# Eight modulation products at once: raising the adaLN units over a recurrence, and adding head sums low part first

## The chip, the cores and the metric

The kernel runs on one core of a Trainium2 chip. The metric is device time in microseconds (us), from the launch's start to its end on that core. A change of 0.3% is 4.9 us.

## The reference

One step of a diffusion backbone: 512 latent tokens and 128 context tokens of width 1024, one layer, all in float32. The layer is a mixer of three bidirectional recurrences (HGRN2, RWKV-7, mLSTM), each with a gated branch projection, and after it a SwiGLU; each half has an RMSNorm in front and behind. Cut to what the change touches:

```python
mod = (jax.nn.silu(cond) @ P['w_ada'][l] + P['b_ada'][l])[:, None, :]     # (2, 6 * 1024): c and c_ctx
sh1, sc1, g1, sh2, sc2, g2 = jnp.split(mod, 6, axis=-1)
h = _rms(x, nw[0]) * (1 + sc1) + sh1
y, st = _mixer(h, ...)                       # z = h @ W_in, 9616 columns, then the three recurrences
x = x + g1 * _rms(y, nw[1])
h = _rms(x, nw[2]) * (1 + sc2) + sh2
...                                          # SwiGLU, then x + g2 * _rms(y, nw[3])
# inside _rwkv7, sums over the 64 channels of each head:
kk = kk / jnp.maximum(jnp.sqrt(jnp.sum(kk * kk, axis=-1, keepdims=True)), 1e-12)
mean = jnp.mean(o, axis=-1, keepdims=True); var = jnp.mean(jnp.square(o - mean), axis=-1, keepdims=True)
bonus = jnp.sum(r_h * k_h * r_k, axis=-1, keepdims=True) * v_h
```

## The kernel before

**Layout and precision.** Channels lie on the 128 partitions, the 640 tokens on the free axis, in halves of 320. A projection of 128 output channels is a tile `pj` of one PSUM bank per token half; each of its 8 blocks of 128 input channels takes three single-pass matmuls (high by high, high by low, low by high parts, each rounded to `fp32r`), so a half has 24 of them.

**Modulation.** `sh1` and `sc1` are needed at once and are done before the mixer by `ada_first`. The other four vectors (32 of 48 blocks of 128 columns) are made by `ada_units`, 16 units of 256 columns, beside the recurrences. A unit loads two 512 KB pieces of `w_ada` (`raw`; the first holds input blocks 0 to 3, the second 4 to 7), and multiplies each of the eight blocks by a stationary of 32 columns (`sc32`, of which two count). Block k goes to quarter k % 4 of the PSUM tile `acc`, so that four products lie side by side in the array, in a shape of 128 x 32, and the second four add to the first. Each product is plain float32 and shows as two PE instructions in the profile: a unit has 16. ScalarE copies `acc` into `rows`, and `ada_columns` turns `rows` into columns and sums the quarters (`col_`, four PE instructions), one unit later.

**What shares a pool.** `acc`, `col_` and all projections take their banks from one pool, `pj`: two banks during the RWKV stage, four in the stage of the other two recurrences. `rows` shares two SBUF buffers (`gs`) with the gate projections, whose results go from `gs` to DRAM. The loads of the units share three `raw` buffers with all weights in the RWKV stage and have two of their own (`rawb`) in the next.

**Order.** Nothing here is queued by hand. A planner walks the program with its own model of times; on each engine it takes the ready instruction that stands earliest in the text. `tc.high_priority(n)` makes instructions count as n places earlier. The buffers and banks of one pool are handed out in the order of the text: in the compiled program all 408 tiles of `pj` are first written in that order. The RWKV chain (`rwkv`) runs 400 places up (`OFFD`), the projections ahead of it (`front_ahead`) and the filling work (`fill`) at their own places. `fill` follows `ORDER`: gate and output projections (h, o, g) with a unit (a) behind every two of them. `visit` keeps the many small matmuls of one chain step together on PE.

**Head sums.** `head_sum` sums over the 64 channels of a head by a matmul with a block matrix of ones, `bones`: ScalarE rounds the argument to `s_hi`, VectorE makes the rest, `s_lo`, and two matmuls add up in a tile `hs`. It is called eight times for each of the four head pairs, in `rwkv_front` and in `rwkv_post` (which runs raised), 32 times in all. Its bank is one of two that the chain's `lr`, `vtr` and `gg` tiles use too.

Of the kernel before, what the change touches and what calls it, by code (L numbers as in the profile page):

```python
# [49 lines left out]
SRATE = (0.3, 0.3, 0.3, 0.3)  # L50
OFFD = 400
OFFF = 0
HRATE = 2.0
KD = 8
C_DECAY = float(np.exp(-0.5))
# [200 lines left out]
def build(tc, **A):  # L256
# [19 lines left out]
    def mm(out, lhsT, rhs, start=True, stop=True, more=False):  # L276
        newest[0] = pe.matmul(out, lhsT=lhsT, rhs=rhs, start=start, stop=stop, skip_group_check=more).ins  # L277
# [12 lines left out]
    def f32(ap):  # L290
        return ap.bitcast(F32)

    with ExitStack() as top:
# [29 lines left out]
        def run(g):  # L323
            for _ in g:
                pass
# [4 lines left out]
        def wload(src, n=1024, pool_=None):  # L330
            raw = (raw_p if pool_ is None else pool_).tile([128, 1024], F32, name="raw")
            sp.dma_start(raw[:, :n], src)
            return raw
# [42 lines left out]
        def mixproj(name, x, evac):  # L376
            if name in loaded:
                wts, accs = loaded.pop(name)
                for n in range(2):
                    half_proj(wts, x, KD, n, evac, accs[n], range(4, KD))  # L380
                    yield
            else:
                yield from proj_steps(wsplit(A["wmix"][MIX_AT[name]]), x, KD, evac)

        def whole(g):

            n = sum(1 for _ in g)
            for _ in range(n):
                yield

        def half(t, n):
            return t[:, n * HN:(n + 1) * HN]
# [11 lines left out]
        sc32 = cp.tile([128, KD, 32], F32, name="sc32")  # L404
        pool.memset(sc32, 0.0)
        pool.tensor_copy(sc32[:, :, 0:2], sc)

        def ada_part(acc, raw, k0, w):


            for a in range(1024 // w):
                k = k0 + a
                q = slice(32 * (k % 4), 32 * (k % 4) + 32)
                mm(acc[q], sc32[:, k], raw[:, a * w:a * w + w], k < 4, k >= 4)

        def ada_columns(o, rows, n):

            col_ = pj_p[0].tile([128, 4, 2], F32, name="col_", tag="pj")
            for m in range(n):
                mm(col_[:, m], rows[:, m * 128:m * 128 + 128], cols[:, COL_SEL:COL_SEL + 2])  # L420
            tt(mod[:, o:o + n], col_[:, :n], P("b_ada", o, n).unsqueeze(2).to_broadcast([128, n, 2]), ALU.add)
# [81 lines left out]
        bones = mc_p.tile([128, 128], F32R, name="bones")  # L503
# [36 lines left out]
        def weave(*streams):  # L540

            live = [[g, r, 0.0] for g, r in streams]
            while live:
                x = min(live, key=lambda a: a[2])
                try:
                    next(x[0])
                    x[2] += 1.0 / x[1]
                    yield
                except StopIteration:
                    live.remove(x)  # L550
# [13 lines left out]
        def fill():  # L564

            def to_dram(i, name, raw=False):
                def ev(acc, n):
                    gs = gt_p.tile([128, HN], F32, name="gs")
                    if raw:
                        act.copy(gs, acc)  # L570
                    else:
                        act.activation(gs, acc, AF.Tanh, scale=0.5)
                    sp.dma_start(half(gates[i], n), gs)
                yield from whole(mixproj(name, h, ev))
                filled.add(i)

            def ada_units():

                last = None
                for u in range(16):  # L580
                    acc = pj_p[0].tile([128, 256], F32, name="acc", tag="pj")
                    for b in range(2):
                        ada_part(acc, wload(A["wada"][16 + 2 * u + b], pool_=ada_raw[0]), 4 * b, 256)
                    if last:
                        ada_columns(*last)
                    rows = gt_p.tile([128, HN], F32, name="rows", tag="gs")
                    act.copy(rows[:, :256], acc)
                    last = (16 + 2 * u, rows, 2)
                    yield
                ada_columns(*last)  # L590
                yield

            au = ada_units()
            todo = {"g": [(b * 8 + m, f"g{b}_{m}") for b in range(3) for m in range(8)],
                    "h": [(28 + i, f"hg{i}", True) for i in range(4)],
                    "o": [(24 + i, f"mo{i}") for i in range(4)], }
            for x in ORDER:
                if x == "a":
                    yield next(au)
                else:  # L600
                    yield from to_dram(*todo[x].pop(0))
            assert not any(todo.values())
            yield from au

        ada_raw = [raw_p]
# [3 lines left out]
        def first(g, offset):  # L609

            while True:
                try:
                    if offset:
                        with tc.high_priority(offset):
                            next(g)
                    else:
                        next(g)
                except StopIteration:
                    return
                yield  # L620

        def run_over(main, under, rate):

            a = 0.0
            for _ in main:
                a += rate[at[0]]
                while a >= 1.0:
                    a -= 1.0
                    next(under, None)
# [5 lines left out]
        with ExitStack() as rs:  # L635
# [296 lines left out]
            def head_sum(b, eng):  # L932

                hi = tp.tile([128, HN], F32R, name="s_hi", bufs=1)
                lo = tp.tile([128, HN], F32R, name="s_lo", bufs=1)
                act.copy(hi, b)
                eng.tensor_tensor(lo, b, f32(hi), ALU.subtract)
                acc = ps.tile([128, HN], F32, name="hs", tag="A")
                mm(acc, bones, hi, True, False)
                mm(acc, bones, lo, False, True)  # L940
                return acc

            def rwkv_front(p, R):
# [16 lines left out]
                for n in range(2):  # L960
                    ts(half(nkk, n), head_sum(half(t1, n), HE), 1e-24, op0=ALU.max)
# [21 lines left out]
                for n in range(2):  # L983
                    mul(half(yb, n), head_sum(half(t2, n), HE), half(v, n))
# [30 lines left out]
            def front_ahead():  # L1015

                for x in fr:
                    yield
                    while at[0] < 3 and Rs[at[0] + 1].get("ready"):
                        yield  # L1020
# [9 lines left out]
            def rwkv():  # L1030
                last = None
                for p in range(4):
                    while not Rs[p].get("ready"):
                        yield next(fr)
                    at[0] = p
                    elem, prepare, scan = rwkv_pair(p, Rs[p])
                    for gi in range(3):
                        g = chain(elem(), prepare(0)) if gi == 0 else prepare(gi)
                        yield from weave((last, SRATE[p]), (g, 1.0)) if last else g
                        last = scan(gi)  # L1040
                        if gi == 2:
                            last = chain(last, finish(p))
                yield from last

            run_over(weave((first(rwkv(), OFFD), 1.0), (first(front_ahead(), OFFF), FRONT)), fl, FILL)

        with ExitStack() as ms, ExitStack() as mr:
# [288 lines left out]
            def mlstm():  # L1336
                yield from mlstm_gates()
                mr.close()
                mt = ms.enter_context(tc.tile_pool(name="mt", bufs=2, reuse_waits="tile"))
                for hd in range(4):  # L1340
                    at[0] = hd
                    yield from mlstm_head(hd, mt)
# [89 lines left out]
            def hgrn():  # L1432
                for hd in range(4):
                    yield from hgrn_head(hd)

            at[0] = 0
            run_over(weave((mlstm(), 1.0), (hgrn(), HRATE)), fl, FILL2)
            run(fl)
# [106 lines left out]
        def ff1_tiles():  # L1545
            return ft.tile([128, T], F32, name="u"), ft.tile([128, T], F32, name="sg")
# [240 lines left out]
        for c, js in enumerate(CHUNKS):  # L1787
# [3 lines left out]
            if c == 0:  # L1791
# [3 lines left out]
                u, sg = ff1_tiles()  # L1795
# [38 lines left out]
```

## Time and profile before

| | us |
|---|---|
| median of the runs shown (1621.6 to 1626.25, three runs) | 1624.72 |
| the profiled execution's own time | 1626.68 |
| its span, from the first to the last instruction | 1624.9 |
| PE busy in the span | 1550.9 (95%) |
| VectorE, ScalarE, GpSimd busy | 1104.1, 802.4, 276.3 |

The span is 1.8 us short of the execution's own time, and that execution lies 2.0 us above the median. PE means matmuls, PEld weight loads, which can run beside them. A matmul's record covers its way through the array, so records overlap; what one instruction costs is read better from the start of one to the start of the next. SP issues the loads; its rows say when, not for how long a transfer ran.

### The profile page before, as it was taken

To read this page: it belongs to the slowest core of one execution; us is meant where nothing else is said; L and a number is where in the kernel's file an instruction comes from. 1 tells how busy PE (TensorE), PEld (TensorE's weight loads), DVE (VectorE), ACT (ScalarE), POOL (GpSimd) and SP (SyncE) were. 2 spreads that over 40 slices of the span, in tenths; PEclk is the share of its full clock that TensorE was granted. 3 is DMA by queue.
4 is the path that set the end of the run, shared out by engine and by line. 5 is a ranking of instruction groups with operands and counts; after the bars stand their busy time and mean duration, and the time that the engine had idled before them with its cause. 6 is when DMAs were issued, how large, how long until landed. Compare 5 with 4: busy or idle time off the path is not lost. (4 is left out here: it accounts for less than half of the span.)

```text
span 1624.9 us, 36010 instructions
## 1 busy us (share of the span) xinstructions
PE 1550.9 (95%) x14834; PEld 1424.6 (88%) x14834; DVE 1104.1 (68%) x2307; ACT 802.4 (49%) x1594; POOL 276.3 (17%) x347
## 2 busy tenths in 40 slices
PE   5999999999999998899999999999999999999996
PEld 2988878878877888889798988999999999999996
DVE  5787767676677544686858678772887386586576
ACT  5354555364455354756476666223553443343244
POOL 1110111110110110221303021000123241341211
PEclk9999999999999999999999999999989999999998
DMA  9221212222223232232332333643512222222322
GB/s 351 81 71 62 83 58 76 68 82 74 67 72 100 88 132 87 61 105 80 90 101 85 99 103 97 200 143 110 156 37 85 95 79 75 82 89 69 102 96 88
DMA packets 63796, 157.43 MB, mean 97 GB/s; under 512 B 7432, under 2 KB 27912, under 8 KB 63504
## 3 DMA queue, kind: packets, MB, share of 16 engines
q1 hardware_dynamic: 63488, 155.13, 29.7%
q8 instruction: 116, 1.90, 0.5%
q14 instruction: 48, 0.39, 0.1%
q10 hardware_dynamic: 144, 0.00, 0.0%
HBM read 136.73 MB, written 18.37 MB: 95 GB/s over the span
## 5 line engine op out<-in xcount | busy, mean ns | idle before, releaser
L277 PE MATMUL pj<-h_hi,whi 128*128 128x320 f32 x1560 | 494.9, 320 | 5.9 <-ACT t L396 2.9
L277 PE MATMUL pj<-h_hi,wlo 128*128 128x320 f32 x1560 | 493.8, 317 | 0.0
L277 PE MATMUL pj<-h_lo,whi 128*128 128x320 f32 x1560 | 493.5, 317 | 0.0
L262 DVE TENSOR_TENSOR wlo<-raw,whi 128x512 fp32r<-128x512 f32 (+1 forms) x318 | 228.4, 726 | 129.8 <-ACT whi L344 104.5
L277 PEld LDWEIGHTS pj<-h_hi,whi 128*128 128x128 f32 x1560 | 295.1, 190 | 13.0 <-ACT t L396 4.2
L277 PEld LDWEIGHTS pj<-h_hi,wlo 128*128 128x128 f32 x1560 | 295.7, 190 | 3.6
L277 PEld LDWEIGHTS pj<-h_lo,whi 128*128 128x128 f32 x1560 | 295.8, 190 | 3.2
L344 ACT CAST whi<-raw 128x512 fp32r<-128x512 f32 (+1 forms) x264 | 156.9, 600 | 215.4 <-PE pj L277 200.8
L277 PE MATMUL pj<-a,whi 128*128 128x320 f32 x704 | 155.3, 309 | 0.0
L277 PEld LDWEIGHTS pj<-a,whi 128*128 128x128 f32 x704 | 117.7, 188 | 0.2
L277 PE MATMUL pj<-a,wlo 128*128 128x320 f32 x352 | 108.8, 309 | 0.0
L277 PE MATMUL pj<-t_hi,whi 128*128 128x320 f32 x288 | 89.1, 309 | 1.1 <-DVE u L262 1.1
L277 PE MATMUL pj<-t_hi,wlo 128*128 128x320 f32 x288 | 89.1, 309 | 0.4 <-DVE wlo L262 0.4
L277 PE MATMUL pj<-t_lo,whi 128*128 128x320 f32 x288 | 89.0, 309 | 0.0
L1686 ACT CAST whi<-sm 128x512 fp32r<-128x512 f32 x72 | 44.4, 621 | 64.5 <-PE pj L277 50.2
L262 DVE TENSOR_TENSOR wlo<-sm,whi 128x512 fp32r<-128x512 f32 x72 | 68.0, 946 | 11.6 <-ACT whi L1686 8.6
L1680 POOL TENSOR_TENSOR sm<-raw 128x512 f32<-128x512 f32 x36 | 48.4, 1346 | 110.7 <-DMA raw<-wff 72.9
L277 PEld LDWEIGHTS pj<-a,wlo 128*128 128x128 f32 x352 | 66.1, 188 | 0.0
L277 PE MATMUL pj<-hl,whi 128*128 128x320 f32 x256 | 56.5, 310 | 0.6 <-ACT hl L1464 0.6
L807 DVE CAST_PREDICATED E<-msk,q 128x512 f16<-128x512 uint8 (+1 forms) x60 | 35.9, 598 | 30.3 <-PE q L277 30.2
L277 PE MATMUL acc<-raw,sc 128*32 128x256 f32 (+1 forms) x320 | 42.1, 454 | 15.0 <-DMA raw<-wada 15.0
L1686 ACT CAST whi<-raw 128x512 fp32r<-128x512 f32 x54 | 33.5, 621 | 45.6 <-PE pj L277 37.7
(661 smaller groups left out, 3029.2 us busy)
## 6 DMA issues: line engine op xcount, KB each, us to landing
raw<-wmix SPq DMA_DIRECT2D x76, 512.0 KB, 3.8
raw<-wada SPq DMA_DIRECT2D x48, 512.0 KB, 4.6
raw<-wff SPq DMA_DIRECT2D x44, 512.0 KB, 3.8
gates<-gs SPq DMA_DIRECT2D x64, 160.0 KB, 1.7
raw<-wff SPq DMA_DIRECT2D x24, 384.0 KB, 3.2
gs<-gates SPq DMA_DIRECT2D x24, 320.0 KB, 3.0
raw<-wbr SPq DMA_DIRECT2D x12, 512.0 KB, 4.0
raw<-wout SPq DMA_DIRECT2D x8, 512.0 KB, 5.0
```

The costliest lines, as they stand in the source:

```text
L262: dve.tensor_tensor(out, a, b, op)
L277: newest[0] = pe.matmul(out, lhsT=lhsT, rhs=rhs, start=start, stop=stop, skip_group_check=more).ins
L344: act.copy(hi[:, :w], raw[:, o:o + w])
L807: dve.copy_predicated(E[l][:, :, :n], mki(l), q[:, :, :n])
L1680: pool.tensor_tensor(o, x, y, op)
L1686: act.copy(hi, x)
```

## The change

The two loads of a unit are both issued ahead of its products. The products then run in one block that counts as 1000 places earlier (the chain has 400): first the four of the second load, which now start the sums, then the four of the first. The copy to `rows` and `ada_columns` keep their places. In `head_sum` the two matmuls change places: the low part starts the sum, the high part ends it. The amount of work is the same. `ada_first` calls `ada_part` as before.

```diff
+OFFA = 1000
@@
-        def ada_part(acc, raw, k0, w):
+        def ada_part(acc, raw, k0, w, first=None):
             for a in range(1024 // w):
                 k = k0 + a
                 q = slice(32 * (k % 4), 32 * (k % 4) + 32)
-                mm(acc[q], sc32[:, k], raw[:, a * w:a * w + w], k < 4, k >= 4)
+                start = k < 4 if first is None else first
+                mm(acc[q], sc32[:, k], raw[:, a * w:a * w + w], start, not start)
@@ ada_units
                     acc = pj_p[0].tile([128, 256], F32, name="acc", tag="pj")
-                    for b in range(2):
-                        ada_part(acc, wload(A["wada"][16 + 2 * u + b], pool_=ada_raw[0]), 4 * b, 256)
+                    parts = [wload(A["wada"][16 + 2 * u + b], pool_=ada_raw[0]) for b in range(2)]
+
+                    with tc.high_priority(OFFA):
+                        for b in (1, 0):
+                            ada_part(acc, parts[b], 4 * b, 256, b == 1)
                     if last:
                         ada_columns(*last)
                     rows = gt_p.tile([128, HN], F32, name="rows", tag="gs")
@@ head_sum
                 acc = ps.tile([128, HN], F32, name="hs", tag="A")
-                mm(acc, bones, hi, True, False)
-                mm(acc, bones, lo, False, True)
+                mm(acc, bones, lo, True, False)
+                mm(acc, bones, hi, False, True)
```

## Rows read from the trace of the kernel before

**Rows 1.** The page: busy time of each engine, and one group of PE instructions (count, then busy us and mean ns of one, then idle time before them).

```profile
PE 1550.9 (95%) x14834; PEld 1424.6 (88%) x14834; DVE 1104.1 (68%) x2307; ACT 802.4 (49%) x1594; POOL 276.3 (17%) x347
...
L277 PE MATMUL acc<-raw,sc 128*32 128x256 f32 (+1 forms) x320 | 42.1, 454 | 15.0 <-DMA raw<-wada 15.0
```

**Rows 2.** Busy time by stage: about the RWKV stage, the HGRN and mLSTM stage, and the rest. Columns: the stretch, its length, busy us (and instructions) of PE, PEld, DVE, ACT and POOL, granted clock, share and GB/s of the DMA engines.

```profile
100.00:600.00 500.00, 490.71 (x6594) 404.29 (x6593) 340.56 (x838) 251.20 (x512) 65.87 (x144) 1.00 0.24 78
600.00:1010.00 410.00, 385.26 (x3742) 363.79 (x3741) 289.70 (x629) 256.45 (x508) 71.86 (x80) 0.99 0.30 92
1010.00:1624.90 614.90, 594.85 (x4025) 591.24 (x4024) 406.39 (x707) 248.82 (x492) 124.28 (x96) 0.97 0.32 101
```

**Rows 3.** The same view, of the instructions that write or read `acc` alone, one stretch for each of the 16 units. Columns: the stretch, its length, busy us of PE (16 instructions each), PEld and ACT, clock, DMA. The last row sums all 16.

```profile
135.00:138.00 3.00, 1.68 (x16) 0.54 (x16) 0.37 (x1) 1.00 0.09 15
...
390.00:392.00 2.00, 1.07 (x16) 0.42 (x16) 0.05 (x1) 1.00 0.14 18
451.00:454.20 3.20, 1.89 (x16) 0.44 (x16) 0.37 (x1) 1.00 0.26 27
483.00:490.50 7.50, 2.29 (x16) 0.67 (x16) 0.30 (x1) 1.00 0.06 22
...
1001.00:1003.00 2.00, 1.07 (x16) 0.42 (x16) 0.00 (x0) 1.00 0.00 0
sum 80.10, PE 27.29 PEld 8.06 ACT 2.19; mean PE 1.71 PEld 0.50 ACT 0.14
```

**Rows 4.** The timeline of PE in the RWKV stage around a unit. Columns: start, us, engine, line, operation, tiles, shape, count, and in brackets the idle time before.

```profile
450.91 0.30 PE L277 MATMUL pj<-h_hi,wlo 128*128 128x320 f32 x1
451.14 0.62 PE L277 MATMUL acc<-raw,sc 128*32 128x256 f32 x2
451.69 0.31 PE L277 MATMUL xp<-c,Y 64*64 64x64 f16 x8
451.93 0.64 PE L277 MATMUL acc<-raw,sc 128*32 128x256 f32 x8
452.50 0.68 PE L277 MATMUL rr<-Xf,NA 64*64 64x64 f32 x16
453.12 0.63 PE L277 MATMUL acc<-raw,sc 128*32 128x256 f32 x6
453.68 0.61 PE L277 MATMUL col__6030<-cols,rows 128*128 128x2 f32 x4
```

**Rows 5.** The timeline of PE around the last unit, in the same columns.

```profile
1001.09 0.31 PE L277 MATMUL pj<-h_lo,whi 128*128 128x320 f32 x1
1001.24 0.31 PE L277 MATMUL pj<-h_hi,wlo 128*128 128x320 f32 x1
1001.48 1.07 PE L277 MATMUL acc<-raw,sc 128*32 128x256 f32 x16
1002.48 0.61 PE L277 MATMUL col__13893<-cols,rows 128*128 128x2 f32 x4
```

**Rows 6.** The timeline of SP: when the loads of the unit of rows 7 were issued; and how long the 48 loads of `w_ada` took to land.

```profile
522.88 0.33 SPq L332 DMA_DIRECT2D raw<-wada  x1
...
524.88 0.33 SPq L332 DMA_DIRECT2D raw<-wada  x1
```
```profile
DMA to landing us min/median/max: 3.5/4.6/10.2
```

**Rows 7.** The timelines of PE, of ScalarE and of VectorE around one unit of the RWKV stage that stands behind a gate projection.

```profile
557.29 0.39 PE L277 MATMUL pj<-h_hi,wlo 128*128 128x320 f32 x1
557.61 0.62 PE L277 MATMUL acc<-raw,sc 128*32 128x256 f32 x2
558.16 0.45 PE L277 MATMUL z<-zs,Yf 64*64 64x64 f32 x8
558.54 1.06 PE L277 MATMUL acc<-raw,sc 128*32 128x256 f32 x14
559.53 0.61 PE L277 MATMUL col__8195<-cols,rows 128*128 128x2 f32 x4
560.60 0.41 PE L277 MATMUL pj<-h_hi,whi 128*128 128x320 f32 x1 [0.46 <-ACT rows L587]
```
```profile
557.84 0.44 ACT L572 ACTIVATE gs<-pj 128x320 f32<-128x320 f32 x1
560.18 0.37 ACT L587 COPY rows<-acc 128x256 f32<-128x256 f32 x1 [1.90 <-PE col__8195 L277]
```
```profile
560.18 0.16 DVE L262 TENSOR_TENSOR mod<-col__8195,pcol 128x4 f32<-128x4 f32 x1 [0.92 <-PE col__8195 L277]
```

**Rows 8.** The timeline of PE around a head sum; one group of VectorE instructions (ns: least, median, most); and one row of the waits of PE (us in total, times, longest).

```profile
401.27 0.41 PE L277 MATMUL hs<-s_hi,bones 128*128 128x320 f32 x1 [0.25 <-ACT s_hi L936]
401.61 0.37 PE L277 MATMUL y<-Y,E 64*64 64x64 f16 x11
401.92 0.41 PE L277 MATMUL hs<-s_lo,bones 128*128 128x320 f32 x1
402.26 0.24 PE L277 MATMUL y<-Y,E 64*64 64x64 f16 x3
```
```profile
L937 DVE TENSOR_TENSOR s_lo<-t,s_hi x24: 450/491/561, 85.5 to 596.6; 128x320 fp32r<-128x320 f32 x24
```
```profile
PE hs L277 <- ACT s_hi L936: 0.4, 2, 0.3
```

## The prediction

> **What bounds the kernel now.** First the busy times of the page [rows 1]: PE is busy 1550.9 of 1624.9 us, the next engine, VectorE, 1104.1. Then the same by stage [rows 2]. The changed instructions lie in the first two stretches: the RWKV stage, where PE lacks 500 - 490.7 = 9.3 us of being always busy, and the next stage, where it lacks 24.7. So there is little waiting to remove, and a change gains only if PE gets the same products done in less time. That this is possible shows in two columns: in the RWKV stage matmuls are busy 490.7 us but weight loads only 404.3, while after 1010 us both are near 594. In the RWKV stage something stands between the matmuls that counts as busy.
>
> What it is shows when the starts of neighbours are compared. Inside a half projection the next matmul starts 0.15 us later ([rows 5], 1001.09 to 1001.24). From the last `pj` matmul to the first of `acc` it is 0.24 (1001.24 to 1001.48). A whole unit in one piece takes 1.00 until the next instruction starts (1001.48 to 1002.48). In [rows 4] a unit is cut into three: 0.55, 0.57 and 0.56 from each piece's start to the start of the foreign work behind it, 1.68 in all. Two instructions cost over half of what sixteen cost together, so most of a piece is the price of getting out of the array's 128 x 32 shape.
>
> **The change, part by part.**
>
> *The loads.* Both are already issued well before they are needed: the pair of [rows 6] at 522.88 and 524.88, with a landing time of 4.6 us in the median and 10.2 at most, for products that start at 557.61 [rows 7]. Starting from the later load and issuing both first therefore costs and gains 0. The cover is some 20 us of lead; without it PE would stand up to 10.2 us at a unit, and nothing in the change removes it, since loads keep their place in the text.
>
> *The products in one piece.* [Rows 3] has the PE time of each unit: 1.07 where it ran whole (two units, at 390 and 1001), 1.68 in two pieces, 1.89 in three, 2.29 in the worst, together 27.29. Sixteen whole units would take 16 x 1.07 = 17.12, which leaves 10.17. A piece's record overlaps the next instruction by 0.07 (451.14 + 0.62 against 451.69), and by their busy times the units have some 36 pieces, 20 more than 16: 20 x 0.07 = 1.4 is no gain. So joining them is worth 10.2 - 1.4 = 8.8 us if no unit is cut any more. It should not be: once the first product can go, the other seven are ready and stand 1000 places up, ahead of the chain's 400. Bounds: 0 if other work still gets between, 8.8.
>
> The Trainium skill ("TensorEngine Tiling (Array Packing)", Key Properties) has a reason for the 0.5 us: a change of tiling mode drains the engine. It gives no price; by it a piece between two kinds of work whose modes differ anyway would save one drain of two, and the sum would be half, 4.4 (a time of 1622.4, a rival below). The rows speak against half: in [rows 4] two `acc` instructions take 0.55 and eight take 0.57, so the price hangs on the exit from `acc`, not on the products, and it goes with the piece.
>
> *Where the products go.* Today all products stand behind the last matmul of the half projection before them, because its matmuls are earlier in the text. At 1000 places up they go as soon as a bank of `pj` is free. In the RWKV stage there are two banks: the one of the first half comes free when that half is evicted, early in the second half. So the products move into the middle of the second half. That takes away a cover. Today they fill the time in which ScalarE evicts the second half: in [rows 7] the eviction ends at 557.84 + 0.44 = 558.28, and PE could go on at 557.61, so 0.67 us is covered. After the change that time belongs to `col_`, which is next in the text for a bank, and it must wait; then the next projection waits for a bank from `col_` (VectorE ends at 560.34, 0.81 after the start of `col_`, of which PE works 0.61) or from `rows`. New uncovered time: 0.67 + 0.20 = 0.87 a unit. The chain's small matmuls fill part of it: `z` holds 0.38 (558.16 to 558.54) of the 0.93 from 557.61 to 558.54, and `xp` and `rr` in [rows 4] are more, so I take half. Eleven units lie in the RWKV stage; six of them stand behind a gate projection, whose `gs` buffer also holds up `rows`, and five behind a projection of the chain, where `rows` can be copied early and the bank is back in time. I take 6 x 0.87 x 0.5 = 2.6, with 0.4 for the five others: 3. Bounds: 0, since today's wait for `rows` (0.46 in [rows 7]) may go with it, and 11 x 0.87 = 9.6 if nothing fills it. The five units of the second stage have four banks and lose nothing.
>
> *Head sums.* The low part is ready one VectorE instruction (0.49 us, [rows 8]) after the high part. Today PE takes the high part as soon as it is there, turns to other work and comes back: in [rows 8] each of the two visits inside the group `y` takes 0.34 until `y` goes on, against 0.15 for a matmul among its like. With the low part first, both are ready when the first goes, so one visit serves both. A visit saved is worth 0.34 - 0.15 = 0.19 or a little more (its way in), and about nothing where the neighbours are `pj`. Read in the same way, 20 of the 32 pairs stand apart in the timeline; at some 0.12 each that is 2.5 us. Bounds: 0, and 20 x 0.19 = 3.8. The bank is taken later and for a shorter time, and `s_hi` is held about 0.5 us longer; the next head sum waits for that, but its 0.5 us lies under PE's other work.
>
> *Sum.* -8.8 + 3 - 2.5 = -8.3 us of PE time, in stages where PE is 94 to 98% busy. The whole order behind the first moved instruction is planned anew, so the 34 us of idle time in these stages may shift by a few us either way; some products that now fall into waits will do so no more. I take -7: the profiled execution's 1626.7 would become 1619.7. It lies 2.0 above the median of the runs, so the median goes from 1624.7 to about 1618.
>
> **The rivals.**
>
> *The full gain, 1612:* no uncovered time and all visits gone, 1624.7 - 8.8 - 3.8. For it: PE shows hardly any wait for banks today. Against: the bank of `acc` is held longer than now.
>
> *No change, 1624:* the products go together, but what they saved is lost again where PE has no bank to write to (bubble of 0.87 little filled, 8 to 9 us) or the new order leaves other pieces cut. For it: two banks, and the wait of 0.46 that is already there. The change not doing what it says, with units still cut, ends here too, and so does the skill's half gain (1622.4, 0.04 of the chance).
>
> *Slower, 1633:* the two banks block each other. `acc` sits in one from the middle of the second half until `rows` is copied, and `rows` needs a `gs` buffer, of which the unit before holds one; the other bank waits for its eviction. If PE stood 1.8 us (0.99 from 557.29 until the eviction's end, and the 0.81 of `col_`) at each of eleven units, that is 19.8 against gains of 11.3, so 1624.7 + 8.5. It decides from 11.3 / 11 = 1.03 us a unit on. Against it: the chain always had matmuls to give around a unit (`xp`, `rr` and `z` in [rows 4, 7]). The Trainium skill ("TensorEngine Tiling (Array Packing)", PSUM Bottleneck) warns of this kind of thing: packing speeds up the products, not the eviction.
>
> *PE stands at the low part, 1632:* the queue of PE holds at a matmul whose operand is late, and the low part is 0.49 later than the high one: 32 x 0.49 = 15.7, less the 8.8 of the products: 1624.7 + 6.9. Against it: PE waited 0.4 us in all at head sums for `s_hi` [rows 8], and the planner places them by when both parts are ready. The Trainium skill ("TensorE: Matmul & The Clock Gate", Part 3, The mechanism) says that matmuls stay in order.
>
> **How the numbers follow.** Forecast (1613 to 1622, most likely 1618) 0.52, full gain 0.06, no change 0.24, banks blocked 0.13, low part late 0.05. What a measurement can tell from no change is 0.3%, 4.9 us: faster is below 1619.8. Of the forecast some four fifths lie there, with the full gain 0.48 and a little of "no change": 0.5. Same: a fifth of the forecast and most of "no change", 0.31. Slower: 0.19, the last two and a rest. The range, 1611 to 1630, leaves out the lower end of the full gain and the worse half of the slower cases.
>
> **What the profile after would show.** Right: `acc` in 16 rows of x16, each about 1.07, sum near 17.1 in the view of [rows 3]; `pj` matmuls of one half on both sides of them in the RWKV stage; `s_lo` directly followed by `s_hi`; PE busy down by some 10 us, its idle time between 100 and 1010 us up by 2 to 4. Wrong: `acc` still in pieces; `pj` or `col_` in the RWKV stage with idle time behind ScalarE's `gs` or `rows` of over 0.5 us at most units; waits of `hs` on `s_lo`; a longer gap between the stages near 650 us.

## The result, and the profile after

The change made the kernel slower: 1636.43 us in the median (8 runs) against 1624.38 for the kernel before, beside it, a ratio of 1.0076 with an interval of 1.0057 to 1.0096. That is 12 us in place of the 7 us of gain forecast, and above the range. The profiled execution after took 1636.35 us, with a span of 1634.5.

The first view is of the products alone, one stretch for each unit, as in [rows 3] (a unit in the middle, and the sum):

```profile
452.00:455.00 3.00, 1.07 (x16) 0.42 (x16) 0.37 (x1) 1.00 0.23 45
...
sum 141.00, PE 17.13 PEld 6.68 ACT 5.59; mean PE 1.07 PEld 0.42 ACT 0.35
```

All sixteen units run whole, in 1.07 us, together 17.13 where [rows 3] has 27.29. The head sums do what was forecast, too: PE's timeline around one (against [rows 8]), and what PE waits for at them in the whole run.

```profile
342.01 0.31 PE L278 MATMUL hs<-s_lo,bones 128*128 128x320 f32 x1
342.16 0.31 PE L278 MATMUL hs<-s_hi,bones 128*128 128x320 f32 x1
```
```profile
PE hs L278 <- DVE s_lo L942: 0.9, 3, 0.4
```

25 of the 32 pairs now stand next to each other (11 before), and waiting for the low part costs 0.9 us in all. So the work has become less, as it should. The page's line for PE and the busy time by stage (as [rows 1] and [rows 2], the same stretches up to 1010 us) show what else happened:

```profile
PE 1545.6 (95%) x14834; PEld 1430.2 (87%) x14834; DVE 1106.9 (68%) x2307; ACT 801.4 (49%) x1594; POOL 278.4 (17%) x347
```
```profile
100.00:600.00 500.00, 483.11 (x6567) 405.21 (x6566) 339.99 (x836) 246.82 (x506) 67.73 (x144) 0.99 0.24 75
600.00:1010.00 410.00, 381.06 (x3722) 361.99 (x3721) 282.70 (x603) 249.82 (x489) 72.43 (x80) 0.98 0.29 91
```

PE's idle time grew from 9.3 to 16.9 us in the RWKV stage and from 24.7 to 28.9 in the next, and the granted clock fell by 0.01 in both. The trace records the clock as stretches at full or at half speed; up to the start of the last stage (the first write of `x1d`, at 1138.9 us before and at 1149.1 after) half-speed stretches last 20.5 us before and 41.0 after. At half speed half the time is lost, which gives an account of the 10.2 us:

| up to the first `x1d` | before | after | difference |
|---|---|---|---|
| time | 1138.9 | 1149.1 | +10.2 |
| PE idle, 100 to 1010 us | 34.0 | 45.8 | +11.8 |
| half of the time at half clock | 10.2 | 20.5 | +10.3 |
| the rest: PE's work at full clock, and its idle time outside 100 to 1010 us | 1094.7 | 1082.8 | -11.9 |

(Each column is one execution, and idle time at half clock counts twice, so each row is good to some 2 us. With all idle time up to the first `x1d`, 54.6 and 68.8, and only busy time at half clock, the differences are +14.1 idle, +10.4 clock and -14.3 work.) The work saved is at least what the prediction said, 8.8 + 2.5 = 11.3. It was paid back by idle time, for which the prediction had 3, and then lost once more to the clock, for which it had nothing. The runs bear the clock out: over 29 runs of the kernel before, the time falls by 1.03 us for each 0.001 of mean granted clock. Its mean was 0.986 in those runs, and 0.979 in the eight of the changed kernel: about 7 of the 12 us.

Where does it happen? First in the RWKV stage, at the unit that starts at 332 us (unit 4). The timeline of PE, that of ScalarE, and the stretches before and after the pause (columns as in [rows 4], [rows 7] and [rows 2]):

```profile
332.41 1.07 PE L278 MATMUL acc<-raw,sc 128*32 128x256 f32 x16
...
343.33 0.31 PE L278 MATMUL pj<-h_hi,wlo 128*128 128x320 f32 x1
344.96 1.16 PE L278 MATMUL p<-AX,BK 64*128 64x128 f32 x8 [1.32 <-DVE BK L263]
346.05 0.80 PE L278 MATMUL col__4607<-cols,rows 128*128 128x2 f32 x4
346.77 2.08 PE L278 MATMUL p<-AX,BK 64*128 64x128 f32 x8
```
```profile
344.81 0.42 ACT L574 ACTIVATE gs<-pj 128x320 f32<-128x320 f32 x1
...
346.88 0.37 ACT L592 COPY rows<-acc 128x256 f32<-128x256 f32 x1 [1.03 <-PE col__4607 L278]
```
```profile
332.00:346.30 14.30, 12.97 (x97) 8.78 (x95) 10.84 (x25) 9.43 (x19) 3.11 (x6) 1.00 0.36 118
346.30:360.00 13.70, 13.70 (x79) 12.12 (x79) 9.04 (x24) 3.96 (x8) 1.65 (x5) 0.50 0.02 7
```

Three things are to be seen. The products ran at 332.41, in the middle of the second half; their result left the bank at 346.88, 14.5 us later, because `rows` got no `gs` buffer: the copy waits for `col__4607`, which reads the `rows` of the unit before. Behind the second half (its last `pj` is at 343.33) the chain is not ready, since VectorE is late with `BK`, and PE has nothing to put in: 1.32 us idle. And from 346.3 the clock is granted at 0.50, 1.2 of 2.4 GHz, for 13.7 us: eight matmuls `p` take 2.08 in place of 1.16.

Second, in the HGRN and mLSTM stage, at units 12 and 14. Unit 12, ScalarE, PE, and the stretch behind it:

```profile
784.42 0.44 ACT L574 ACTIVATE gs<-pj 128x320 f32<-128x320 f32 x1 [3.38 <-DMA gates<-gs]
784.75 0.58 ACT L1145 COPY hkt<-htr 128x512 f32<-128x512 f32 x1
```
```profile
781.90 0.31 PE L278 MATMUL pj<-h_lo,whi 128*128 128x320 f32 x1
785.39 1.16 PE L278 MATMUL hpr<-hv,hkt 128*128 128x128 f32 x8 [3.18 <-ACT hkt L1145]
```
```profile
786.70:790.00 3.30, 3.30 (x18) 3.30 (x17) 2.83 (x7) 1.66 (x4) 1.65 (x2) 0.50 0.38 144
```

The second half's `gs` stands in ScalarE's queue in front of the chain's `hkt`, and waits 3.38 us until the DMA of the `gs` before it has left the buffer. PE waits 3.18 for `hkt`, and the clock is at half behind that. At unit 14 it is the same (3.21, 3.02, half clock from 974.4). In the kernel before, `hkt` stands in front of that `gs` (ScalarE at the same unit):

```profile
776.23 0.58 ACT L1140 COPY hkt<-htr 128x512 f32<-128x512 f32 x1
779.44 0.44 ACT L572 ACTIVATE gs<-pj 128x320 f32<-128x320 f32 x1 [2.63 <-DMA gates<-gs]
```

The wait for the DMA is there too, 2.63 us, but PE loses only 1.49 us to it, at the `mkt` that stands behind that `gs`.

### The profile page after: what moved, and what is told of

Same layout as the page of the kernel before. It is cut to its first block, busy times and chain, and to the rows that moved or that the text cites. A ratio compares the mean times of both kernels' runs of the same rounds, so it can differ in the third digit from the quotient of the medians.

```text
span 1634.5 us, 36013 instructions
## 1 busy us (share of the span) xinstructions
PE 1545.6 (95%) x14834; PEld 1430.2 (87%) x14834; DVE 1106.9 (68%) x2307; ACT 801.4 (49%) x1594; POOL 278.4 (17%) x347
## 5 line engine op out<-in xcount | busy, mean ns | idle before, releaser
L812 DVE CAST_PREDICATED E<-msk,q 128x512 f16<-128x512 uint8 (+1 forms) x60 | 35.9, 598 | 30.8 <-PE q L278 30.6
L278 PEld LDWEIGHTS pj<-t_hi,whi 128*128 128x128 f32 x288 | 54.1, 188 | 1.3 <-DVE u L263 1.3
```

The costliest lines, as they stand in the source:

```text
L812: dve.copy_predicated(E[l][:, :, :n], mki(l), q[:, :, :n])
```

## The experiments

All are compared with the kernel before, run beside them (medians 1624.3 to 1625.6). The account is that of the table above, of the one profiled execution of each; "rest" is against the kernel before. Some of these executions are not typical: that of e_early (1622.0 us) and that of e_tailnow (1609.7) were the fastest of their runs, that of e_own (1625.7) the slowest.

| run | median us | ratio, interval | idle 100 to 600, 600 to 1010 | half of half clock | rest |
|---|---|---|---|---|---|
| e_ada | 1634.92 | 1.0070 (1.0046 to 1.0093) | 14.8, 29.6 | 20.5 | -9.3 |
| e_hs | 1620.78 | 0.9976 (0.9963 to 0.9989) | 9.5, 23.9 | 10.2 | -3.9 |
| e_off0 | 1623.68 | 0.9996 (0.9982 to 1.0011) | 10.4, 23.8 | 10.2 | +1.2 |
| e_tail | 1618.53 | 0.9966 (0.9951 to 0.9982) | 12.8, 27.4 | 10.2 | -13.0 |
| e_late | 1622.78 | 0.9992 (0.9982 to 1.0003) | 12.9, 31.3 | 15.4 | -15.2 |
| e_early | 1626.48 | 1.0014 (1.0002 to 1.0025) | 17.0, 26.0 | 11.9 | -11.3 |
| e_alt | 1635.84 | 1.0055 (1.0033 to 1.0077) | 16.1, 29.8 | 27.3 | -13.5 |
| e_now | 1638.41 | 1.0095 (1.0080 to 1.0111) | 18.3, 30.6 | 25.6 | -14.2 |
| e_tailnow | 1614.48 | 0.9938 (0.9923 to 0.9954) | 11.4, 26.1 | 5.1 | -10.8 |
| e_tailmod | 1619.51 | 0.9967 (0.9952 to 0.9981) | 12.8, 28.0 | 13.7 | -15.6 |
| e_own | 1621.40 | 0.9971 (0.9956 to 0.9986) | 12.8, 25.8 | 22.2 | -13.4 |
| e_ownlate | 1611.89 | 0.9918 (0.9896 to 0.9941) | 11.0, 26.1 | 13.7 | -14.9 |
| e_u4 | 1630.24 | 1.0044 (1.0027 to 1.0061) | 16.2, 30.6 | 15.4 | -11.7 |
| e_u1214 | 1630.44 | 1.0034 (1.0022 to 1.0047) | 16.7, 26.4 | 15.4 | -11.4 |

**Which part costs.** Four kernels take the change apart. e_ada:

```diff
-                mm(acc, bones, lo, True, False)
-                mm(acc, bones, hi, False, True)
+                mm(acc, bones, hi, True, False)
+                mm(acc, bones, lo, False, True)
```

> The changed kernel with the head sums of before (high part first), so the products alone are changed. If the place of the products is what costs (the bank theory: in the RWKV stage acc now sits in one of two banks of pj until rows finds a gs buffer, PE runs dry, and the clock falls after it), this run keeps the loss: 1638, with acc holding its bank 8 us and more behind gate projections, and events at half clock near units 4, 12 and 14. If the head sums are what costs (the rival), the loss goes: 1622 or less.

e_hs is the kernel before with these lines exchanged:

```diff
-                mm(acc, bones, hi, True, False)
-                mm(acc, bones, lo, False, True)
+                mm(acc, bones, lo, True, False)
+                mm(acc, bones, hi, False, True)
```

> The kernel before with the two matmuls of a head sum exchanged and nothing else. Bank theory: the head sums are a small gain, 1622 (my forecast for them was 2.5 us), pairs lo and hi next to each other. Rival (PE stands at the low part): 1630 to 1636, with waits of hs on s_lo of several us in all.

e_tail, with `q0(k)` for the product of block k:

```diff
+                    q0(4)
                     with tc.high_priority(OFFA):
-                        for b in (1, 0):
-                            ada_part(acc, parts[b], 4 * b, 256, b == 1)
+                        for k in (5, 6, 7, 0, 1, 2, 3):
+                            q0(k)
```

> The changed kernel, but of the eight products of a unit the first counts at its own place in the text and only the other seven are raised. So the products are still joined (sixteen whole units), but stand behind the last matmul of the second half projection, as before. Bank theory: the moved place is the loss, the joining a gain, so this is faster than both: 1613 to 1617, acc 1.0 us a unit, no more idle time of PE in the RWKV stage than before. Rival (joining or starting from the later load, or any new order of the plan, is what costs): 1630 to 1637.

e_off0:

```diff
-OFFA = 1000
+OFFA = 0
```

> The changed kernel with the raise set to 0: both loads issued first, the products from the later load on, at their own place in the text, head sums low part first. The units are cut into pieces again. Bank theory: the time of before or a little less, 1620 to 1625, since neither the place nor the joining is left. Rival (the order of the loads and products itself costs): 1630 to 1637.

e_ada keeps the loss (+10.3 us), e_hs gains 3.9, e_tail gains 6.1, e_off0 comes out as before. So neither the head sums, nor the joining, nor the order of the loads costs on balance: the place of the products does. Two expectations were off. In e_ada the half clock that was expected near units 4, 12 and 14 came near 14 alone; 41.0 us of it are there up to the first `x1d` all the same, most of them elsewhere in the two stages. And e_tail's idle time in the RWKV stage did grow, by 3.5 us (by 2.7 in the next), and of the 9.1 us by which its rest lies below that of e_hs only 2.3 reach the median. e_off0 cuts the units into 44 pieces (37 in the kernel before, 32 in e_hs), and its head sums gain nothing on balance. Nor do they in the changed kernel: e_ada, which has the old order, is no slower (1634.92 against 1636.43).

**Which stage.** e_late and e_early take the products of one stage back to the old place (`late` in the diff is `u < 11` in the first and `u >= 11` in the second):

```diff
+                    if late:
+                        q0(4)
                     with tc.high_priority(OFFA):
-                        for b in (1, 0):
-                            ada_part(acc, parts[b], 4 * b, 256, b == 1)
+                        for k in (4, 5, 6, 7, 0, 1, 2, 3)[late:]:
+                            q0(k)
```

> Units 0 to 10 (the RWKV stage) as in e_tail, with the first product at its own place; units 11 to 15 (the HGRN and mLSTM stage) raised as in the changed kernel. It shows what the moved place costs in the second stage alone. Of the 18 us between e_tail (1618.5) and the changed kernel (1636.4) I put 7 there: two waits of PE of about 3 us for hkt, held up in ScalarE's queue behind a gs that waits for its DMA, and the fall of the clock behind them; so 1625. Rival (what I predicted: four banks, nothing lost there): 1618 to 1619.

> The other half: units 0 to 10 raised as in the changed kernel, units 11 to 15 as in e_tail. It shows what the moved place costs in the RWKV stage alone. By the trace 11 of the 18 us (idle time of PE up by 7.6 in the stretch from 100 to 600 us, and 13.65 us at half clock at unit 4): 1629. Rival (nothing lost in the second stage): 1636. If the two losses are independent, e_late and e_early lie as far above e_tail together as the changed kernel does.

The moved place costs 4.3 us over e_tail in the second stage alone and 8.0 in the RWKV stage alone. Together that is 12.3 of the 17.9 between e_tail and the changed kernel. With the clock's part taken out they add up: to the first `x1d`, time less half of the half-clock time lies 1.9 and 4.5 us above e_tail, and for the changed kernel 6.8. What is more than additive is clock. The mean clock of all runs points the same way: 0.984 in e_tail, 0.983 and 0.984 in these two, 0.979 in the changed kernel.

**Is it the bank?** The first suspect in the RWKV stage was the bank that `acc` holds for 14.5 us. e_alt gives half the units a tile of their own:

```diff
-                    rows = gt_p.tile([128, HN], F32, name="rows", tag="gs")
+                    if u < 10 and u % 2 == 0:
+                        rows = lw.tile([128, 256], F32, name="rows")
+                    else:
+                        rows = gt_p.tile([128, HN], F32, name="rows", tag="gs")
```

> The changed kernel, but in the RWKV stage the units 0, 2, 4, 6 and 8 copy acc into a tile of their own instead of a gs buffer, so that rows of these units, and of the units behind them, finds a buffer at once. (A tile of its own for every unit does not fit.) If the shortage of gs buffers is what keeps acc in its bank (9 to 14 us behind gate projections), the hold falls to 1 to 3 us, PE has its banks, and most of the loss of the RWKV stage goes: 1626 to 1628. Rival (the two banks block each other anyway, because col_ and the next projection must wait for the eviction of the second half): 1633 to 1637 with the holds short.

Its PE and ScalarE timelines at unit 4, and ScalarE's at unit 7:

```profile
330.66 1.07 PE L278 MATMUL acc<-raw,sc 128*32 128x256 f32 x16
```
```profile
331.80 0.37 ACT L595 COPY rows<-acc 128x256 f32<-128x256 f32 x1 [1.45 <-PE acc L278]
...
487.82 0.44 ACT L574 ACTIVATE gs<-pj 128x320 f32<-128x320 f32 x1
488.15 0.37 ACT L595 COPY rows<-acc 128x256 f32<-128x256 f32 x1
```

At unit 4 the bank is free 1.5 us after the products began, and the clock falls there all the same (half speed from 344.5). At unit 7 the copy still stands behind the second half's `gs`, 14 us after the products. The median did not move, and the holds were gone only in part. But the runs fall into two groups, six of 1635.8 to 1640.3 us (mean clock 0.976 to 0.979) and four of 1626.4 to 1628.6 (0.984 to 0.986), so this run alone settles nothing. e_now tried it in another way:

```diff
-                    if last:
-                        ada_columns(*last)
                     rows = gt_p.tile([128, HN], F32, name="rows", tag="gs")
-                    act.copy(rows[:, :256], acc)
-                    last = (16 + 2 * u, rows, 2)
+                    with tc.high_priority(OFFA):
+                        act.copy(rows[:, :256], acc)
+                    ada_columns(16 + 2 * u, rows, 2)
                     yield
-                ada_columns(*last)
-                yield
```

> The changed kernel, but acc is copied to rows at raised priority right behind the products, and ada_columns follows in the same unit instead of one unit later. So no gs buffer is held from unit to unit, the gates have both, and acc leaves its bank after 1 to 2 us. If the shortage of gs buffers is what costs (in the RWKV stage by the held bank, in the second stage by the gs that waits in ScalarE's queue for its DMA, in front of hkt), the holds are short, the two waits of 3 us for hkt and the falls of the clock behind them are gone, and the time is 1618 to 1624. Rival (the cover that the products gave behind the second half is what is missing, whatever the buffers do): the RWKV stage keeps its idle time, 1630 to 1636.

It did not do what it was made for. Buffers go out in the order of the text, so `rows` comes behind the second half's `gs` whatever its priority, and now has the wait for the DMA itself (ScalarE and PE at unit 12):

```profile
788.38 0.37 ACT L591 COPY rows<-acc 128x256 f32<-128x256 f32 x1 [3.26 <-DMA gates<-gs]
788.65 0.59 ACT L1142 COPY hkt<-htr 128x512 f32<-128x512 f32 x1
```
```profile
788.80 1.01 PE L278 MATMUL col__11277<-cols,rows 128*128 128x2 f32 x4 [3.60 <-ACT rows L591]
```

So it says nothing on the bank; for the second stage it shows that another instruction that waits for that DMA in front of `hkt` leaves PE idle about as long (3.60 us against 3.18). e_own settles the bank of `acc` in the RWKV stage; e_ownlate is its control (it has `if True` for `if not rwkv`, and `[1:]` for `[not rwkv:]`):

```diff
+                    rwkv = u < 11
+                    if not rwkv:
+                        q0(4)
                     with tc.high_priority(OFFA):
-                        for b in (1, 0):
-                            ada_part(acc, parts[b], 4 * b, 256, b == 1)
-                    if last:
-                        ada_columns(*last)
-                    rows = gt_p.tile([128, HN], F32, name="rows", tag="gs")
-                    act.copy(rows[:, :256], acc)
-                    last = (16 + 2 * u, rows, 2)
+                        for k in (4, 5, 6, 7, 0, 1, 2, 3)[not rwkv:]:
+                            q0(k)
+                    if rwkv:
+                        rows = lw.tile([128, 256], F32, name="rows")
+                        with tc.high_priority(OFFA):
+                            act.copy(rows, acc)
+                    else:
+                        rows = gt_p.tile([128, HN], F32, name="rows", tag="gs")
+                        act.copy(rows[:, :256], acc)
+                    ada_columns(16 + 2 * u, rows, 2)
                     yield
-                ada_columns(*last)
-                yield
```

> In the RWKV stage (units 0 to 10) the products raised as in the changed kernel, but with a tile of their own for rows, its copy raised right behind the products, and ada_columns in the same unit; the second stage as in e_tailnow. So in the RWKV stage acc is in the middle of the second half and yet leaves its bank after some 1.5 us at every unit, which e_alt and e_now did not reach. Against e_tailnow (1614.5) it differs by the place of the products in the RWKV stage alone. If the held bank is what the place costs, nothing is left of it: 1613 to 1616. If the cost is that the products no longer run behind the second half, where PE else has nothing, the idle time of PE between 100 and 600 us stays at 14 to 17 us and the time is 1620 to 1625.

> The control for e_own: the same tile for rows, the same raised copy, ada_columns in the same unit, and the products of all units at their old place behind the second half (first product at its own place, seven raised). By both theories about e_tailnow: 1613 to 1616, with some 10 us of idle time of PE between 100 and 600 us. If it lies at 1620 or more, the new tile or the raised copy itself costs, and e_own must be read against this run.

e_own at unit 4 (PE, ScalarE, and the stretch that begins 15 us later):

```profile
331.99 1.07 PE L278 MATMUL acc<-raw,sc 128*32 128x256 f32 x16
...
344.91 0.41 PE L278 MATMUL pj<-h_hi,whi 128*128 128x320 f32 x1 [0.81 <-ACT gs L574]
...
346.41 2.80 PE L278 MATMUL p<-AX,BK 64*128 64x128 f32 x16 [0.36 <-DVE BK L263]
```
```profile
333.12 0.37 ACT L596 COPY rows<-acc 128x256 f32<-128x256 f32 x1 [0.93 <-PE acc L278]
```
```profile
347.30:360.90 13.60, 13.60 (x85) 12.59 (x85) 9.44 (x25) 3.96 (x8) 2.44 (x5) 0.50 0.00 1
```

Here `rows` is copied 1.1 to 1.5 us after the start of the products at every unit of the RWKV stage, and the moved place still costs 9.5 us against e_ownlate: 1621.4 to 1611.9. The bank that `acc` holds is not what costs. In front of the fall at unit 4 PE here waits 0.81 us for ScalarE's `gs`, the eviction of the second half, and 0.36 for `BK`; in e_ownlate, with the products behind the second half, it idles 0.23 us in all from 342 to 354. The idle time in the RWKV stage differs by 1.8 us only (my 14 to 17 were too many), the half-clock loss by 8.5. e_ownlate in the same stretch:

```profile
347.30:360.90 13.60, 13.60 (x219) 11.60 (x217) 10.74 (x25) 6.49 (x14) 1.75 (x4) 1.00 0.38 119
```

The same time holds 219 instructions of PE here and 85 there (not the same ones, as unit 4 runs at 350.2 here). e_ownlate has the lowest median of all, 13.4 us below the kernel before beside it.

**Two more tries at a better kernel.** Both start from e_tail. e_tailnow:

```diff
-                    if last:
-                        ada_columns(*last)
                     rows = gt_p.tile([128, HN], F32, name="rows", tag="gs")
                     act.copy(rows[:, :256], acc)
-                    last = (16 + 2 * u, rows, 2)
+                    ada_columns(16 + 2 * u, rows, 2)
                     yield
-                ada_columns(*last)
-                yield
```

> The same with the products at their old place as in e_tail (first product at its own place, seven raised) and the copy of acc not raised: ada_columns in its own unit. It is the control for e_now and a try at a better kernel. If holding a gs buffer costs with the old place too, it beats e_tail: 1614 to 1616. If col_ now waits for rows with nothing to cover it (0.37 us of copy a unit and the way to and from ScalarE), 1620 to 1625.

e_tailmod:

```diff
-            tt(mod[:, o:o + n], ...
+            with tc.high_priority(OFFA):
+                tt(mod[:, o:o + n], ...
```

> e_tail with VectorE's sum of col_ into mod at raised priority, so that the bank of col_ comes free at once (in e_tail mod comes 9.3 us behind col_ at unit 7 and 25 us at unit 11). If that bank is missed by the next projections, 1614 to 1616; if not, the time of e_tail, 1618.5.

e_tailnow gains 4.1 us over e_tail, and by the account it is clock (10.2 to 5.1) and 2.7 us of idle time, not work; the mean clock of all runs, 0.988 against 0.984, agrees. Its interval overlaps that of e_ownlate, so the two can't be told apart. e_tailmod gains nothing: that bank was not missed.

**By what the place costs.** Two kernels put single units back, with the diff of e_late (`late` is `u == 4`, and `u in (12, 14)`); the order of all other units stays as in the changed kernel.

> The changed kernel with unit 4 alone back at its old place (first product at its own place, seven raised); the order of all other units stays. In the trace of the changed kernel PE has a pause of 1.32 us behind the second half of that unit (it waits for VectorE's BK), 1.4 us later the granted clock falls to half for 13.65 us, and in the kernels with the old place no fall is seen there. If the missing cover is the cause, the products fill that pause, the fall goes, and the time is 6 to 8 us less: 1628 to 1631. If the fall has nothing to do with the pause: 1635 to 1637.

> The changed kernel with units 12 and 14 alone back at their old place. In the changed kernel's trace these are the two where ScalarE's gs waits 3.4 and 3.2 us for its DMA in front of hkt, PE waits 3.2 and 3.0 us for hkt, and the clock falls for 3.41 us behind each. In this kernel hkt stands in front of that gs again. If these two places are the loss of the second stage: 4 to 8 us less, 1629 to 1632. If the waits come back elsewhere in the stage: 1634 to 1637.

e_u4 at unit 4, PE and the stretch behind:

```profile
343.74 0.31 PE L278 MATMUL pj<-h_hi,wlo 128*128 128x320 f32 x1
343.98 1.07 PE L278 MATMUL acc<-raw,sc 128*32 128x256 f32 x16
344.98 0.61 PE L278 MATMUL col__4607<-cols,rows 128*128 128x2 f32 x4
346.11 1.16 PE L278 MATMUL p<-AX,BK 64*128 64x128 f32 x8 [0.52 <-DVE BK L263]
```
```profile
346.30:360.00 13.70, 13.70 (x181) 12.12 (x181) 12.18 (x31) 5.91 (x13) 2.61 (x6) 1.00 0.30 100
```

VectorE is as late with `BK` as in the changed kernel, but the products now fill the time; 0.52 us of waiting is left, and the clock stays at 1.00. One unit moved back is worth 6.2 us in the median, and by the account it is clock (20.5 to 15.4): idle time in sum and work stay within 1 us of the changed kernel's. But five of its twelve runs lie at 1634.8 to 1637.9, where those of the changed kernel lie, with a mean clock of 0.976 to 0.982; where it fell in them no trace shows. The mean of all runs is 4.6 us lower, with a clock of 0.982 against 0.979.

e_u1214 at unit 12, ScalarE and PE:

```profile
779.42 0.59 ACT L1148 COPY hkt<-htr 128x512 f32<-128x512 f32 x1
782.56 0.44 ACT L574 ACTIVATE gs<-pj 128x320 f32<-128x320 f32 x1 [2.56 <-DMA gates<-gs]
```
```profile
779.86 1.07 PE L278 MATMUL acc<-raw,sc 128*32 128x256 f32 x16
780.86 1.16 PE L278 MATMUL hpr<-hv,hkt 128*128 128x128 f32 x8
```

`hkt` is in front of `gs` again, and the products run while ScalarE copies it: no wait of PE, and no fall of the clock behind either unit. That is worth 6.0 us. The account gives 2.7 of idle time and 5.1 of clock up to the first `x1d`, but the mean clock of all its runs is hardly higher, 0.980 against 0.979, so how the gain splits stays open. The two gains add up to the 12 us that the change lost, but no run puts all three units back at once.

## Why the prediction was wrong

- *Products in one piece, -8.8, and head sums, -2.5:* right in sum, as work: 11.9 us less by the account (forecast 11.3). The products came to 17.13 (forecast 17.12), and e_ada, which has them alone, has 9.3 less. The head sums can't be told apart so well: e_hs gained 3.9 us, but PE's busy time in it, counted at full clock, is only 0.4 us less up to the first `x1d` (what is left of its -3.9 is idle time), and in the changed kernel they gain nothing in the median. "PE stands at the low part" is ruled out: 0.9 us of waits.
- *Loads, 0:* nothing in the runs speaks against it, but no run tests it alone.
- *Uncovered time, +3 (bounds 0 to 9.6):* this step failed, in size and in mechanism. I priced one known gap per unit, ScalarE's eviction of the second half, and filled half of it with the chain. That gap shows in e_own, 0.81 us at unit 4. But the cover that the products gave was mostly not for the eviction. They were loose work, lying ready behind the second half when the chain had none: at unit 4 while VectorE was late with `BK`, at units 12 and 14 while ScalarE copied `hkt`. Idle time rose by 7.6 us in the RWKV stage, inside the bounds but two and a half times the 3, and by 4.2 in the next, where I had none. Not all of the 11.8 comes from the place: e_tail, with the products joined behind the second half, has 6.2 more than the kernel before, and the move adds 5.6. Joined products fill fewer waits than pieces do; I had named that, and put 1.3 us on it (-8.3 taken as -7). My own sign for this step, idle time behind `gs` or `rows` of over 0.5 us at most units, did not appear: five waits for `rows` of 0.46 to 0.78 us are there, and the long ones are on the chain's own operands, `BK` and `hkt` among them.
- *"The five units of the second stage have four banks and lose nothing":* wrong, by 4.3 us in e_late. I counted the banks and left out the queue of ScalarE, in which moving the products put `gs` with its DMA wait in front of `hkt`. I had reckoned with the shortage of `gs` buffers, but for the RWKV stage only.
- *The clock:* missing from the sum altogether, and some 7 to 10 us. It could have been read: [rows 2] has 0.99 and 0.97, and the kernel before shows the pattern at 678 us, where PE waits 4.98 us for `hkt` (these lines of the kernel before were not among its rows):

```profile
678.24 2.07 PE L277 MATMUL hpr<-hv,hkt 128*128 128x128 f32 x8 [4.98 <-ACT hkt L1140]
```
```profile
677.70:681.00 3.30, 2.76 (x12) 2.76 (x13) 2.33 (x5) 1.64 (x4) 0.00 (x0) 0.50 0.10 21
```

- *The rival "Slower, 1633":* near in time (1636), and its picture is in the trace, with `acc` 14.5 us in a bank. But it is not the reason, and the nearness is luck: e_own frees the bank in the RWKV stage and still lies 9.5 us above e_ownlate.

What stays open: of the 9.5 us between e_own and e_ownlate, idle time and rest make 1.5 each by the account, and the mean clock of their runs (0.984 and 0.987) about 4 at 1.03 us for each 0.001; some 3 us I can't place. (The 8.5 us of half clock above are from the slowest execution of e_own.) And the fall at unit 4 is likely, not certain: the profiled execution of e_early has the same order of instructions there, a pause of 1.33 us and no fall; e_ada has such a pause there, too, and no fall.

## What to carry to other kernels

Work that is ready and that nobody waits for is a filler: before moving it forward, look in the timeline at what runs beside it now, on every engine, and which waits it hides; a filler used early leaves those waits bare. Joining scattered pieces and moving them are two changes: e_tail has the first without the second, and e_ownlate, which also has a buffer of its own for the copy and `ada_columns` in the same unit, makes 1612 of it. And where PE is the bound, price a new pause twice: once as idle time, and once as the half clock that can follow.

## What the runs showed of the hardware

A pause can cost far more than its length through the granted clock: 1.32 us of waiting at unit 4 stood in front of 13.7 us at half speed, some 6.8 us lost. In the stretch of unit 4 a fall is seen in 5 of the 7 profiled kernels with the moved place and in none of the 9 with the old one; at unit 12 in 4 of 6 against none of 10, at unit 14 in 6 of 6 against 1 of 10. But a pause is not enough: in the changed kernel PE idles 1.48 us at 271.7 and 1.39 at 325.3, and stays at full clock behind both:

```profile
271.80:275.80 4.00, 4.00 (x65) 3.37 (x66) 3.00 (x8) 0.26 (x1) 0.00 (x0) 1.00 0.37 131
325.30:330.00 4.70, 4.70 (x67) 3.91 (x68) 4.14 (x11) 1.30 (x5) 0.73 (x2) 1.00 0.00 0
```

In e_ada the first of these places has a pause of 1.62 us and a fall of 3.4 us from 270.9. What makes one pause bring a fall and another not was not tried. The Trainium skill ("TensorE: Matmul & The Clock Gate", Part 1: The HAM clock gate) says that the throttled clock is the default and activity lifts it; the stretches at 0.50 behind pauses agree with that.
